# Weight and activation tiles at other byte offsets in SBUF, and high and low parts of one activation in one tile

## The chip, the cores and the metric

The kernel runs on one core of one Trainium2 chip. The metric is the device time of one execution in microseconds (us). Engines are TensorE (PE; its weight loads are shown apart as PEld), VectorE (DVE), ScalarE (ACT), GpSimd (POOL) and SyncE (SP), which issues the transfers. SBUF is the on-chip memory of 128 partitions from which PE reads both operands of a matmul; results go to PSUM. An address below is a byte offset within a partition.

## What is computed

A stack over 256 tokens of width 1,024, batch 1: one block of two mixing layers over 272 tokens (16 meta tokens in front), then two blocks of feed-forward, hybrid mixer, feed-forward, and a last norm. Cut to what matters here:

```python
def first_block(x, meta_tokens, ...):            # 16 + 256 tokens
    h = concat([meta, x]); 
    h = h + even_layer(rms_norm(h))              # latent attention + banded attention, gated, w_out
    h = h + odd_layer(rms_norm(h))               # conv + linear recurrence, gated, w_out
    return h[:, 16:]

def swiglu(x, w_gate, w_up, w_down):             # 1024 -> 2816 -> 1024, four times in all
    return (jax.nn.silu(x @ w_gate) * (x @ w_up)) @ w_down
# then twice: x += swiglu(norm(x)); x += hybrid(norm(x)); x += swiglu(norm(x))
# hybrid: causal pooling branch + gated recurrence over chunks of 64, gates and output projections
```

All inputs and the output are float32.

## The kernel before

Activations stand transposed: features on the 128 partitions, tokens along the free dimension. A projection from 1,024 features is a chain of eight tiles k of 128 features, accumulated in one PSUM bank. Each tile is multiplied with three float32r matmuls (a rounded float32 form that PE takes), so that the result keeps float32's exactness: every operand is cut into a high part and the rest, and the products are `hi·xh`, `hi·xl` and `lo·xh`, in this order (`prod`, line 447). The weights are stationary, the activation is moving:

```python
self.mm(out=out, lhsT=hi if i < 2 else lo, rhs=(xl if i == 1 else xh)[:, k, cols], ...)
```

Weights arrive by SP as `raw` buffers of 2,048 columns (two of them), and are cut into buffers of 1,024 columns, four `hi` and four `lo` (five each from the first feed-forward block's start, `more_cuts`): ACT copies `raw` to `hi`, DVE subtracts to `lo` (`cut`). Activations are cut in the same way (`split`), the normed input of a layer into `xh` and `xl`, 8 tiles of 272 tokens. From the odd layer's output on there are 256 tokens, and `place` (line 503) lays 8 tiles of 256 tokens over the same memory as `sh`, `sl`, from element 32 (`X_AT`).

The stages, in order of time: even layer (272 columns; `xh`/`xl`, the latents `lath`/`latl`, the gated heads `ysh`/`ysl` and `ymh`/`yml`); odd layer (`oyh`/`oyl`; its gates take 256 of the 272 columns); then twice feed-forward (`ffn`, line 1355: gate/up on `sh`/`sl`, down on `ph`/`pl`), hybrid (`hybrid`, line 1471: `hh`, `hl`, `hph`, `hpl`, `mh`, `ml`) and feed-forward; the final norm. In the profile the moving name stands first: `acc<-xl,hi` is a product with `xl` moving and `hi` stationary. The packed `sh`/`sl` show as `xh`, `xl`, whose memory they use. Every instruction goes through a wrapper at line 181, so lines tell nothing and names and shapes do.

The order of the instructions is set while the program is written: a clock with estimated costs (`Clock`, line 120) decides when side work, cuts and loads are put between the products. It looks at names and ranges within tiles, not at addresses. Tiles lie in SBUF one behind the other in the order in which their pool gets them, and `gap` (line 264) puts an unused tile between two to shift what follows.

Of the kernel before, what the change touches and what calls it, by code (L numbers as in the profile page):

```python
# [9 lines left out]
F32 = mybir.dt.float32  # L10
# [6 lines left out]
P = 128  # L17
D = 1024
NM = 16
S = 256  # L20
# [206 lines left out]
class Builder:  # L227

    AHEAD = 3
    X_AT = 32  # L230
    gaps = 0

    def __init__(self, ctx, tc, a):
        self.clock = Clock()
        self.ctx, self.tc, self.nc, self.a = ctx, tc, Core(tc.nc, self.clock), a
        nc = self.nc
        self.tt, self.ts, self.stt, self.ttr = nc.vector.tensor_tensor, nc.vector.tensor_scalar, nc.vector.scalar_tensor_tensor, nc.vector.tensor_tensor_reduce
        self.act, self.mm = nc.scalar.activation, nc.tensor.matmul
        self.cos, self.done, self.cur, self.lists, self.home, self.stalls = [], {}, None, {}, {}, 0
        self.loads = weight_plan()  # L240
        self.plan = [(n, i, ps, p) for n, i, ps in self.loads for p in range(len(ps))]
        self.load_at = self.conv_at = self.use_at = 0
        self.raws, self.conv = [], {}
        self.const = self.pool(ctx, "const")
        self.res = self.pool(ctx, "res", 2)
        psum = self.pool(ctx, "psum", space=PSUM)
        self.make(psum, "acc", 2, [P, 512])
        self.make(psum, "m", 6, [P, 512])
        self.make(self.const, "raw", 2, [P, 2048])
        self.make(self.const, "hi", 4, [P, 1024], F32R)  # L250
        self.make(self.const, "lo", 4, [P, 1024], F32R)
        self.make(self.const, "work", 8, [P, T + 4])
        self.make(self.const, "mx", 6, [P, 16])
# [10 lines left out]
    def gap(self, pool, n):  # L264

        if n:
            self.gaps += 1
            pool.tile([P, n // 4], F32, tag=f"gap{self.gaps}", name=f"gap{self.gaps}")

# [224 lines left out]
    def feed(self, gen, d, x, g, n):  # L494
        if n == S:
            self.place(gen)
            self.split(x, self.sh[:, d, :], self.sl[:, d, :], g)
        else:
            self.split(x, self.xh[:, d, :n], self.xl[:, d, :n], g)
        self.put("x", gen, d)  # L500
        self.spawn(self.square(gen, d, x, n))

    def place(self, gen):

        at = self.X_AT
        self.sh, self.sl = [t.rearrange("p k t -> p (k t)")[:, at:at + KD * S].rearrange("p (k t) -> p k t", t=S) for t in (self.xh, self.xl)]

# [74 lines left out]
    def setup(self):  # L582
# [8 lines left out]
        self.x = self.t(self.const, [P, KD, T], "x")  # L591
        self.xh = self.t(self.const, [P, KD, T], "xh", F32R)
        self.xl = self.t(self.const, [P, KD, T], "xl", F32R)
        nc.vector.memset(self.half, -0.5)
# [5 lines left out]
    def even(self):  # L600
# [67 lines left out]

        lath = self.t(ea, [P, 5, T], "lath", F32R)
        latl = self.t(ea, [P, 5, T], "latl", F32R)  # L670
        sums = {}
# [214 lines left out]

        ys = [self.t(ys_p, [P, 8, T], "ysh", F32R), self.t(ys_p, [P, 8, T], "ysl", F32R)]
        ym = []
# [180 lines left out]
        for h in range(8):  # L1069
            self.spawn(head(h))  # L1070
            if h == 2:
                self.need("early over")
                early.close()
                ymp = self.pool(st, "eym")
                ym += [self.t(ymp, [P, 8, T], "ymh", F32R), self.t(ymp, [P, 8, T], "yml", F32R)]
                self.put("ym")
            ps = self.take("acc")
            self.run(ein(16 + h, ps))
            self.spawn(gate(h, ps), ps)
# [21 lines left out]
    def odd(self):  # L1101
# [23 lines left out]
        def decay_rates():  # L1125
# [21 lines left out]
            self.put("c8")  # L1147

        yh = [self.t(od, [P, G, S], f"oyh{i}", F32R) for i in range(2)]
        yl = [self.t(od, [P, G, S], f"oyl{i}", F32R) for i in range(2)]  # L1150
        xcs, zgs = {}, {}
# [159 lines left out]
        for kind, g in odd_order():  # L1311
# [21 lines left out]
            else:  # L1333
                if g == 0:
                    outs += self.take("m", 4)
                    for o in outs:
                        mm(out=o, lhsT=zero, rhs=xh.rearrange("p k t -> p (k t)")[:, :512], start=True, stop=False)
                if g < 2 * NG - 2:
# [16 lines left out]
    def ffn(self, name, layer, gen, nxt):  # L1355
# [7 lines left out]
        rh = self.rh  # L1363
        self.gap(ff, 160)
        ph = self.t(ff, [P, KFF, S], "ph", F32R)
        pl = self.t(ff, [P, KFF, S], "pl", F32R)

# [61 lines left out]
    def more_cuts(self):  # L1429

        late = self.pool(self.ctx, "late")
        for n in ("hi", "lo"):
            self.lists[n].append(self.t(late, [P, 1024], n + "4", F32R))
        self.AHEAD = 4
# [36 lines left out]
    def hybrid(self, layer, gen):  # L1471
# [7 lines left out]
        hy = self.pool(st, "hy")  # L1479
        self.gap(hy, 32)  # L1480
        self.make(hy, "kq", 2, [P, H, S])
# [30 lines left out]
        pr = self.t(hy, [P, 6, S], "pr")  # L1512
        hh, hl = self.t(hy, [P, H, S], "hh", F32R), self.t(hy, [P, H, S], "hl", F32R)
        ph, pl = self.t(hy, [P, H, S], "hph", F32R), self.t(hy, [P, H, S], "hpl", F32R)

# [228 lines left out]
        for c in HYBRID:  # L1744
# [8 lines left out]
            pair(e, dst[:, e - e0:e - e0 + 2, :], (name, gen, e - e0))  # L1753

        mh, ml = self.t(hy, [P, KD, S], "mh", F32R), self.t(hy, [P, KD, S], "ml", F32R)

# [253 lines left out]
```

## Time and profile before

| | |
|---|---|
| three runs | 1537.36, 1539.48 and 1546.85 us; median 1539.48 |
| profiled execution, its own time | 1542.62 us |
| its span, first to last instruction | 1540.5 us |
| mean granted TensorE clock over the span | 0.996 |
| PE busy | 1507.8 us, 98% of the span, 12,950 instructions |
| DVE busy | 1115.9 us, 72% |
| ACT busy | 904.9 us, 59% |
| HBM read | 256.07 MB, 167 GB/s over the span |

The profile shows one execution, by instruction. Matmuls overlap: one lasts some 0.28 us, and the next starts some 0.11 us after it, so the pace is to be read from how many lie in a stretch, and not from the length of one. A granted clock of 1.00 is the 2.4 GHz level.

### The profile page before, as it was taken

Reading aid. Unit: us, or ns where it says so; the run is one execution under the profiler, and the core shown is the slowest. Engines: PE = TensorE matmul, PEld = TensorE weight load, DVE = VectorE, ACT = ScalarE, POOL = GpSimd, SP = SyncE. Lnnn points to the kernel's source line nnn. Section 1 sums busy time; section 2 is a strip of 40 time slices with the busy share of each in tenths; the row PEclk is TensorE's granted clock in tenths of the full one; section 3 lists DMA queues with packets and bytes.
Section 4 is the critical chain, followed back from the end, with each engine's and each line's share of the span. In section 5 each row is a group of like instructions: output and inputs, shape, how many; then the busy total and the mean of one; then the engine's idle time right before and its main releaser. Section 6 shows DMA issues by size and latency. Waiting matters only on the chain.

```text
span 1540.5 us, 31049 instructions
## 1 busy us (share of the span) xinstructions
PE 1507.8 (98%) x12950; PEld 1473.7 (96%) x12950; DVE 1115.9 (72%) x1882; ACT 904.9 (59%) x1435; POOL 26.2 (2%) x68
## 2 busy tenths in 40 slices
PE   8999999999989999999999999999999998999998
PEld 8989899999989999989999999999999998999998
DVE  6977775689996666668886666666666787777754
ACT  7666654699966545475455544455455754555453
POOL 1000000000000000000000000000000000000000
PEclk9999999999999999999999999999999999999999
DMA  6422224554445645644355555556456433456553
GB/s 240 152 90 83 84 81 164 182 174 143 156 174 189 218 167 183 211 161 165 137 195 189 196 177 174 194 194 214 161 188 209 167 138 137 163 189 222 175 174 117
DMA packets 42492, 259.12 MB, mean 168 GB/s; under 512 B 4840, under 2 KB 6256, under 8 KB 18416
## 3 DMA queue, kind: packets, MB, share of 16 engines
q1 hardware_dynamic: 40624, 251.90, 47.1%
q10 hardware_dynamic: 1728, 5.24, 1.0%
q8 instruction: 101, 1.65, 0.4%
q14 instruction: 39, 0.32, 0.1%
HBM read 256.07 MB, written 1.05 MB: 167 GB/s over the span
## 4 chain that ended last, share of the span: by engine, by line
PE 63%; issue 19%; DVE 10%; ACT 5%; DMA 2%; POOL 0%; POOLq 0%; ACTq 0%; SPq 0%; DVEq 0%
PE acc L181 51%; PE m L181 12%; DVE lo L181 4%; DVE big L181 3%; ACT hi L181 2%; DMA raw<-in_hin_dram 1%; ACT L181 1%; DVE kq L181 1%; ACT big L181 1%; ACT w L181 0%; DVE xc L181 0%; ACT xx L181 0%; DVE xx L181 0%; DMA raw<-in_ffn_gu_dram 0%; DVE work L181 0%
## 5 line engine op out<-in xcount | busy, mean ns | idle before, releaser
L181 DVE TENSOR_TENSOR lo<-raw,hi 128x1024 fp32r<-128x1024 f32 (+3 forms) x520 | 582.7, 1129 | 258.5 <-ACT hi L181 254.8
L181 ACT ACTIVATE hi<-raw 128x1024 fp32r<-128x1024 f32 (+3 forms) x520 | 502.2, 980 | 297.0 <-PE acc L181 207.8
L181 PE MATMUL acc<-xh,hi 128*128 128x256 f32 (+1 forms) x2096 | 589.7, 281 | 5.4 <-ACT hi L181 5.4
L181 PE MATMUL acc<-xl,hi 128*128 128x256 f32 (+1 forms) x2096 | 590.5, 282 | 0.0
L181 PE MATMUL acc<-xh,lo 128*128 128x256 f32 (+1 forms) x2096 | 588.7, 281 | 0.1
L181 PEld LDWEIGHTS acc<-xh,hi 128*128 128x128 f32 x2096 | 394.5, 188 | 6.8 <-ACT hi L181 5.4
L181 PEld LDWEIGHTS acc<-xl,hi 128*128 128x128 f32 x2096 | 395.6, 189 | 1.4
L181 PEld LDWEIGHTS acc<-xh,lo 128*128 128x128 f32 x2096 | 394.6, 188 | 1.6 <-DVE lo L181 0.5
L181 PE MATMUL acc<-pl,hi 128*128 128x256 f32 x704 | 196.9, 280 | 0.0
L181 PE MATMUL acc<-ph,lo 128*128 128x256 f32 x704 | 196.6, 279 | 0.0
L181 PE MATMUL acc<-ph,hi 128*128 128x256 f32 x704 | 196.4, 279 | 0.0
L181 PEld LDWEIGHTS acc<-pl,hi 128*128 128x128 f32 x704 | 132.2, 188 | 0.0
L181 PEld LDWEIGHTS acc<-ph,hi 128*128 128x128 f32 x704 | 132.2, 188 | 0.0
L181 PEld LDWEIGHTS acc<-ph,lo 128*128 128x128 f32 x704 | 131.8, 187 | 0.0
L181 PE MATMUL m<-xh,lo 128*128 128x256 f32 (+1 forms) x336 | 96.0, 286 | 0.0
L181 PE MATMUL m<-xl,hi 128*128 128x256 f32 (+1 forms) x336 | 95.6, 284 | 0.0
L181 PE MATMUL m<-xh,hi 128*128 128x256 f32 (+1 forms) x336 | 95.5, 284 | 0.0
L181 DVE TENSOR_TENSOR work<-acc,spread 128x256 f32<-128x256 f32 (+1 forms) x108 | 46.0, 426 | 38.0 <-PE acc L181 35.3
L181 ACT ACTIVATE work<-work 128x256 f32<-128x256 f32 (+2 forms) x92 | 37.4, 408 | 51.9 <-DVE work L181 51.5
L181 PEld LDWEIGHTS m<-xh,lo 128*128 128x128 f32 x336 | 63.6, 189 | 0.3
L181 PEld LDWEIGHTS m<-xh,hi 128*128 128x128 f32 x336 | 63.6, 189 | 0.2
L181 PEld LDWEIGHTS m<-xl,hi 128*128 128x128 f32 x336 | 63.5, 189 | 0.1
(359 smaller groups left out, 2242.4 us busy)
## 6 DMA issues: line engine op xcount, KB each, us to landing
raw<-in_ffn_gu_dram SPq DMA_DIRECT2D x88, 1024.0 KB, 4.9
raw<-in_ffn_dn_dram SPq DMA_DIRECT2D x64, 704.0 KB, 4.1
raw<-in_hin_dram SPq DMA_DIRECT2D x32, 1024.0 KB, 4.9
raw<-in_oin_dram SPq DMA_DIRECT2D x16, 1024.0 KB, 5.0
raw<-in_ein_dram SPq DMA_DIRECT2D x12, 1024.0 KB, 4.7
raw<-in_eout_dram SPq DMA_DIRECT2D x8, 1024.0 KB, 4.9
raw<-in_oout_dram SPq DMA_DIRECT2D x8, 1024.0 KB, 4.9
raw<-in_wph_dram SPq DMA_DIRECT2D x8, 1024.0 KB, 4.9
```

The costliest lines, as they stand in the source:

```text
L181: r = f(*args, **kw)
```

## The change

The instructions of every engine, their order, shapes and waits stay as they are. What changes is where tiles lie. The high and low part of one activation become two views of one tile: for 272 columns tile by tile (high k, low k, high k+1, ...), by `twins` or by the new `xs`; for 256 columns one half behind the other. Gaps shift the `lo` weight buffers by 192 bytes against the `hi` ones, and the low parts of moving operands by 64 against their high parts. The core of the diff:

```diff
         self.make(self.const, "hi", 4, [P, 1024], F32R)
+        self.gap(self.const, 192)
         self.make(self.const, "lo", 4, [P, 1024], F32R)
...
+    def twins(self, pool, shape, tag):
+
+        k, n = shape
+        t = self.t(pool, [P, k, 2, n], tag, F32R)
+        return t[:, :, 0, :], t[:, :, 1, :]
...
-        at = self.X_AT
-        self.sh, self.sl = [t.rearrange("p k t -> p (k t)")[:, at:at + KD * S].rearrange("p (k t) -> p k t", t=S) for t in (self.xh, self.xl)]
+        self.sh, self.sl = [self.xs[:, at:at + KD * S].rearrange("p (k t) -> p k t", t=S) for at in (0, KD * S + 16)]
...
-        self.xh = self.t(self.const, [P, KD, T], "xh", F32R)
-        self.xl = self.t(self.const, [P, KD, T], "xl", F32R)
+        self.gap(self.const, 192)
+        self.xs = self.t(self.const, [P, 2 * KD * T], "xs", F32R)
+        pairs = self.xs.rearrange("p (k two t) -> p k two t", two=2, t=T)
+        self.xh, self.xl = pairs[:, :, 0, :], pairs[:, :, 1, :]
...
-        lath = self.t(ea, [P, 5, T], "lath", F32R)
-        latl = self.t(ea, [P, 5, T], "latl", F32R)
+        lath, latl = self.twins(ea, (5, T), "lat")
...
-        ys = [self.t(ys_p, [P, 8, T], "ysh", F32R), self.t(ys_p, [P, 8, T], "ysl", F32R)]
+        ys = self.twins(ys_p, (8, T), "ys")
...
+        self.gap(od, 64)
         yh = [self.t(od, [P, G, S], f"oyh{i}", F32R) for i in range(2)]
+        self.gap(od, 64)
         yl = [self.t(od, [P, G, S], f"oyl{i}", F32R) for i in range(2)]
...
-        self.gap(ff, 160)
+        self.gap(ff, 96)
         ph = self.t(ff, [P, KFF, S], "ph", F32R)
+        self.gap(ff, 64)
         pl = self.t(ff, [P, KFF, S], "pl", F32R)
...
-        for n in ("hi", "lo"):
-            self.lists[n].append(self.t(late, [P, 1024], n + "4", F32R))
+        self.gap(late, 128)
+        self.lists["hi"].append(self.t(late, [P, 1024], "hi4", F32R))
+        self.gap(late, 192)
+        self.lists["lo"].append(self.t(late, [P, 1024], "lo4", F32R))
...
-        self.gap(hy, 32)
+        self.gap(hy, 96)
...
+        hh, ph, mh = [self.t(hy, [P, n, S], tag, F32R) for tag, n in (("hh", H), ("hph", H), ("mh", KD))]
+        self.gap(hy, 64)
+        hl, pl, ml = [self.t(hy, [P, n, S], tag, F32R) for tag, n in (("hl", H), ("hpl", H), ("ml", KD))]
```

Where the built programs put these tiles, as addresses modulo 256 bytes (k is the tile of 128 features; a tile of 256 columns is 1,024 bytes and one of 272 is 1,088, which is 64 more than a multiple of 256):

| operand | role | before | after |
|---|---|---|---|
| `hi` 0 to 4 | stationary | 128 | 128 |
| `lo` 0 to 4 | stationary | 128 | 64 |
| `xh`, `xl` as 256 columns | moving, gate/up and hybrid | 64, 64 | 64, 128 |
| `ph`, `pl` | moving, down | 192, 192 | 64, 128 |
| `hh`, `hph`, `mh`; `hl`, `hpl`, `ml` | moving, hybrid | 64; 64 | 64; 128 |
| `oyh`, `oyl` | moving, odd layer | 64, 64 | 64, 128 |
| `xh`, `xl` as 272 columns | moving, even and odd layer | 192+64k, 192+64k | 64+128k, 128+128k |
| `ysh`, `ysl`; `ymh`, `yml` | moving, even layer | 64+64k for all | 192+128k, 128k |
| `lath`, `latl` | moving, even layer | 64+64k, 128+64k | 192+128k, 128k |

PE's first products of the program, in the even layer, in the order in which they stand before (numbers behind a name tell its buffers apart):

```order
L181 MATMUL acc_64<-xh,hi_74 128x272
L181 MATMUL acc_64<-xl,hi_74 128x272
L181 MATMUL acc_64<-xh,lo_78 128x272
L181 MATMUL acc_65<-xh,hi_74 128x272
L181 MATMUL acc_65<-xl,hi_74 128x272
L181 MATMUL acc_65<-xh,lo_78 128x272
```

The same products after the change, on PE, where `xs` is the tile that holds both parts and x2 means two rows with the same names:

```order
L181 MATMUL acc_64<-xs,hi_74 128x272 x2
L181 MATMUL acc_64<-xs,lo_79 128x272
L181 MATMUL acc_65<-xs,hi_74 128x272 x2
L181 MATMUL acc_65<-xs,lo_79 128x272
L181 MATMUL m_66<-xs,hi_74 128x272 x2
```

Only the names differ: `xh` and `xl` have become `xs`, and `lo` buffers are numbered one higher, since a gap stands before them. The same holds where the first feed-forward block goes over from gate/up to down on PE, before:

```order
L181 MATMUL acc_65<-xh,hi_75 128x256
L181 MATMUL acc_65<-xl,hi_75 128x256
L181 MATMUL acc_65<-xh,lo_79 128x256
L181 MATMUL acc_64<-ph,hi_76 128x256
L181 MATMUL acc_64<-pl,hi_76 128x256
L181 MATMUL acc_64<-ph,lo_80 128x256
```

And after, at the same place:

```order
L181 MATMUL acc_65<-xs,hi_75 128x256 x2
L181 MATMUL acc_65<-xs,lo_80 128x256
L181 MATMUL acc_64<-ph,hi_76 128x256
L181 MATMUL acc_64<-pl,hi_76 128x256
L181 MATMUL acc_64<-ph,lo_81 128x256
```

Nothing has moved here either: three products, the same banks and the same weight buffers.

## Rows read from the trace of the kernel before

**Rows 1.** The page's first part: busy time, share of the span and instructions by engine.

```profile
PE 1507.8 (98%) x12950; PEld 1473.7 (96%) x12950; DVE 1115.9 (72%) x1882; ACT 904.9 (59%) x1435; POOL 26.2 (2%) x68
```

**Rows 2.** The page's costliest groups: busy us, mean ns | idle before, its releaser.

```profile
L181 DVE TENSOR_TENSOR lo<-raw,hi 128x1024 fp32r<-128x1024 f32 (+3 forms) x520 | 582.7, 1129 | 258.5 <-ACT hi L181 254.8
L181 ACT ACTIVATE hi<-raw 128x1024 fp32r<-128x1024 f32 (+3 forms) x520 | 502.2, 980 | 297.0 <-PE acc L181 207.8
```

**Rows 3.** Windows of PE alone in the four gate/up stages; x is the matmul count.

```profile
core 0: us, PE busy (x), PEclk, DMA share, GB/s
480.00:560.00 80.00, 80.00 (x708) 1.00 0.59 207
...
825.00:925.00 100.00, 100.00 (x852) 1.00 0.54 189
...
1010.00:1100.00 90.00, 90.00 (x797) 1.00 0.60 208
...
1370.00:1460.00 90.00, 90.00 (x796) 1.00 0.56 197
```

**Rows 4.** The same view, PE alone, in the first and last of four down stages.

```profile
585.00:635.00 50.00, 50.00 (x426) 1.00 0.58 194
...
1475.00:1525.00 50.00, 50.00 (x426) 1.00 0.51 171
```

**Rows 5.** Timeline, gate/up of the first feed-forward block: start, length (us), engine, instruction.

```profile
500.05 0.28 PE L181 MATMUL m<-xh,lo 128*128 128x256 f32 x1
500.05 0.19 PEld L181 LDWEIGHTS m<-xh,hi 128*128 128x128 f32 x1
500.16 0.28 PE L181 MATMUL m<-xh,hi 128*128 128x256 f32 x1
```

**Rows 6.** Windows of PE: even layer (272 columns), odd layer's gates, hybrid, hybrid.

```profile
235.00:285.00 50.00, 50.00 (x399) 1.00 0.53 188
314.50:325.00 10.50, 10.50 (x91) 1.00 0.29 101
708.50:720.00 11.50, 11.50 (x103) 1.00 0.11 26
755.00:810.00 55.00, 55.00 (x488) 1.00 0.54 187
```

**Rows 7.** The page's DMA issues: queue, kind, count, KB each, us to landing.

```profile
raw<-in_ffn_gu_dram SPq DMA_DIRECT2D x88, 1024.0 KB, 4.9
raw<-in_ffn_dn_dram SPq DMA_DIRECT2D x64, 704.0 KB, 4.1
raw<-in_hin_dram SPq DMA_DIRECT2D x32, 1024.0 KB, 4.9
raw<-in_oin_dram SPq DMA_DIRECT2D x16, 1024.0 KB, 5.0
...
raw<-in_oout_dram SPq DMA_DIRECT2D x8, 1024.0 KB, 4.9
raw<-in_wph_dram SPq DMA_DIRECT2D x8, 1024.0 KB, 4.9
```

**Rows 8.** PE groups by line and shape, 272 columns (of three products, one row each).

```profile
L181 PE MATMUL acc<-xh,hi 128*128 128x272 f32 x280 | 85.0, 304 | 5.4 <-ACT hi L181 5.4
...
L181 PE MATMUL m<-xh,hi 128*128 128x272 f32 x104 | 30.7, 295 | 0.0
...
L181 PE MATMUL acc<-ysh,hi 128*128 128x272 f32 x48 | 14.1, 294 | 0.0
```

**Rows 9.** Timeline, hybrid: four products of 512 columns, the first and the last.

```profile
663.74 0.39 PE L181 MATMUL m<-hi,xh 128*128 128x512 f32 x1
...
664.42 0.39 PE L181 MATMUL m<-hi,xh 128*128 128x512 f32 x1
```

**Rows 10.** Timeline, hybrid: a run of one-column matmuls, over two lengths of window.

```profile
735.63 1.39 PE L181 MATMUL m<-cst,kq 128*128 128x1 f32 x12
735.63 0.61 PE L181 MATMUL m<-cst,kq 128*128 128x1 f32 x5
```

More of the change, by code (lines that the diff above doesn't have):

```diff
@@ L229 @@
     AHEAD = 3
-    X_AT = 32
     gaps = 0
@@ L264, in gap @@
     def gap(self, pool, n):
-        if n:
-            self.gaps += 1
-            pool.tile([P, n // 4], F32, tag=f"gap{self.gaps}", name=f"gap{self.gaps}")
+        self.gaps += 1
+        pool.tile([P, n // 4], F32, tag=f"gap{self.gaps}", name=f"gap{self.gaps}")
+    def twins(self, pool, shape, tag):
+        k, n = shape
+        t = self.t(pool, [P, k, 2, n], tag, F32R)
+        return t[:, :, 0, :], t[:, :, 1, :]
     def make(self, pool, name, n, shape, dt=F32):
@@ L495, in feed @@
         if n == S:
-            self.place(gen)
+            self.place()
             self.split(x, self.sh[:, d, :], self.sl[:, d, :], g)
@@ L501, in feed, with place @@
         self.spawn(self.square(gen, d, x, n))
-    def place(self, gen):
-        at = self.X_AT
-        self.sh, self.sl = [t.rearrange("p k t -> p (k t)")[:, at:at + KD * S].rearrange("p (k t) -> p k t", t=S) for t in (self.xh, self.xl)]
+    def place(self):
+        self.sh, self.sl = [self.xs[:, at:at + KD * S].rearrange("p (k t) -> p k t", t=S) for at in (0, KD * S + 16)]
     def square(self, gen, d, x, n):
@@ L1074, in even @@
                 ymp = self.pool(st, "eym")
-                ym += [self.t(ymp, [P, 8, T], "ymh", F32R), self.t(ymp, [P, 8, T], "yml", F32R)]
+                ym += self.twins(ymp, (8, T), "ym")
                 self.put("ym")
@@ L1336, in odd @@
                     for o in outs:
-                        mm(out=o, lhsT=zero, rhs=xh.rearrange("p k t -> p (k t)")[:, :512], start=True, stop=False)
+                        mm(out=o, lhsT=zero, rhs=self.xs[:, :512], start=True, stop=False)
                 if g < 2 * NG - 2:
@@ L1512, in hybrid @@
         pr = self.t(hy, [P, 6, S], "pr")
-        hh, hl = self.t(hy, [P, H, S], "hh", F32R), self.t(hy, [P, H, S], "hl", F32R)
-        ph, pl = self.t(hy, [P, H, S], "hph", F32R), self.t(hy, [P, H, S], "hpl", F32R)
+        hh, ph, mh = [self.t(hy, [P, n, S], tag, F32R) for tag, n in (("hh", H), ("hph", H), ("mh", KD))]
+        self.gap(hy, 64)
+        hl, pl, ml = [self.t(hy, [P, n, S], tag, F32R) for tag, n in (("hl", H), ("hpl", H), ("ml", KD))]
         def memory():
@@ L1753, in hybrid @@
             pair(e, dst[:, e - e0:e - e0 + 2, :], (name, gen, e - e0))
-        mh, ml = self.t(hy, [P, KD, S], "mh", F32R), self.t(hy, [P, KD, S], "ml", F32R)
         def branch_gates():
```

## Prediction

> **What bounds the kernel now.** I read the page's busy times first: TensorE (PE) is busy 98% of a span of 1540.5 us [rows 1], so the end moves only with the pace of PE's own instructions or with its 33 us of idle time. VectorE and ScalarE come next, and they cut the weights: one pair of 1,024-column `hi`/`lo` buffers costs DVE 1.13 us and ACT 0.98 us in the mean, with 258 and 297 us of idle time ahead of such rows, in which they mostly wait for each other or for PE to free a buffer [rows 2]. A pair feeds 24 products (8 tiles of 128 columns, three products each), some 2.7 us of PE. So neither is the limit.
>
> Then I asked what pace PE keeps. The windows by stage, PE alone, give the matmuls that lie in a stretch in which PE never pauses. A matmul row is 0.28 us long while the next starts 0.11 us later [rows 5], so about 2.5 are in flight at the first instant of a window and are counted on top; I take 2.5 off each count (2.3 for 272 columns). The four gate/up stages of the feed-forward blocks issue the same 1,056 products each, from the same buffers, at a granted clock of 1.00, the 2.4 GHz level. Their paces are [rows 3]:
> - 80.00/(708−2.5) = 113.4 ns, 90.00/(797−2.5) = 113.3 and 90.00/(796−2.5) = 113.4 in three of them
> - 100.00/(852−2.5) = 117.7 ns in the second.
>
> Nothing waits there, and the second stage's DMA share (0.54) lies below that of the other three (0.56 to 0.60). So one and the same product has two paces, and a whole stage keeps one of them. The down stages are at the slow pace in all four blocks: 50.00/(426−2.5) = 118.1 [rows 4], where one matmul more or less in the count is 0.3 ns, so I put them at 117.7. What differs between up and down is where the moving operand lies: by the address table 64 bytes below the weights, modulo 256, in up (64 against 128) and 64 above them in down (192 against 128). In the 272-column stage, where the moving operand walks through all four quarters from tile to tile, a product takes 50.00/(399−2.3) = 126.0 ns [rows 6]. 256 columns at 2.4 GHz are 106.7 ns and 272 are 113.3, so what stands over the columns is 6.7, 11.0 and 12.7 ns. The timeline shows what could collide: the next LDWEIGHTS starts within some ns of each MATMUL [rows 5], so one tile's moving rows and the next tile's weights are read from SBUF at once. I read the two paces as this collision, and placement as what the change is about.
>
> **The change part by part.** No engine gets an instruction more or less, none changes place or shape, and no wait is added: the order of the two kernels differs in names only. So every term is pace. The work: a 1,024 KB weight transfer is 16 weight tiles of 128 columns, 48 products; one of 704 KB is 11, 33 products [rows 7]. Gate/up: 88×48 = 4,224. Down: 64×33 = 2,112. The other 256-column products: (32+8+16+8)×48 = 3,072. With 272 columns: 3×(280+104) on `x` and 6×48 on `ys`/`ym`, 1,440 [rows 8].
>
> After the change the moving operand of one product and the weights that are loaded under it stand, product by product, 64 below (`xh` while the `hi` of the second product is loaded), 64 above (`xl` while `lo` is loaded) and 64 below (`xh` while the next `hi` is loaded). They are never level, and the sign changes from product to product. In before it is the same sign for every product of a stage, and the trace shows a stage that stays slow for all of its products. I take it that a slow pace needs the same relation again and again, so that the alternation ends it, and price every 256-column product at the fast pace, 113.4 ns. This step is an inference; its other ends are the rivals.
> - Down stages, 2,112×(117.7−113.4) = −9.1 us.
> - The second gate/up stage, 1,056×4.3 = −4.5 us; the three others nothing.
> - The other 3,072: their three windows give 10.50/(91−2.5) = 118.6, 11.50/(103−2.5) = 114.4 and 55.00/(488−2.5) = 113.3 [rows 6], mean 115.4; 3,072×2.0 = −6.1 us.
> - The 1,440 of 272 columns. Best case: a 512-column product takes (664.42−663.74)/3 = 227 ns [rows 9], so a column costs (227−117.7)/256 = 0.43 ns and 16 columns 6.8, and 113.4+6.8 = 120.2 ns. Worst case: 126.0 as now, since the tiles still walk, now in steps of 128 over two quarters. No row is nearer to either; I take the middle, 123: −4.3 us (ends 0 and −8.4).
> - The 156 latent products and the few with operands exchanged: below 1 us either way, nothing.
>
> Sum −24.0. The profiled execution took 1542.62 us, so 1518.6 on its scale; it stands 3.1 above the median of 1539.48, so about 1516 against that median.
>
> The cutting hides under this as before: 24 products at 113.4 ns are 2.72 us against 1.13 and 0.98. Transfers too: a 1,024 KB raw buffer per 48 products (5.4 us) is what three gate/up stages already drew, 207 GB/s without a pause [rows 3]. If that cover were gone, PE would show idle time before `hi` or `lo`. The gaps cost room and no instruction.
>
> **Rivals.**
> *Little or nothing moves.* If each product's pace goes by its own pair alone, two of three pairs are like up in before (113.4) and one like down (117.7): 114.8 everywhere. Then down and the second gate/up stage gain 3,168×2.9 = 9.2, the rest 3,072×0.6 = 1.8, and the other three lose 3,168×1.4 = 4.4; −6.6 us, about 1533. For it: up and down do differ by this sign. Against it: the second gate/up stage had the same sign as the other three. In the same case belongs that SBUF placement does nothing and the two paces come from elsewhere, an order of start-up for instance that holds for a stage: 1539.5. For that: the one stage with two paces at the same addresses. The Trainium skill has a rule of this kind: "SBUF — State Buffer", section "SBUF: two separate sides", says that of the engines only the pair of ports shared with GpSimd causes contention and that "PE, ACT, and DVE's dedicated pair never wait on anyone". By that rule the time would stay 1539.5; the trace bears on it only in that one product has two paces at full clock with nothing waiting, which the rule leaves without a cause.
>
> *Slower.* The stationary and moving reads of one product are now level in two of three: `xl` lies on the quarter of `hi` and `xh` on that of `lo` (128 and 64). In before the feed-forward stages have no level product. If the product's own pair counts and not the next load, the alternation locks every product at the slow pace. Three gate/up stages then lose 3,168×4.3 = 13.6 us and the rest 3,072×2.3 = 7.1: +20.7, about 1560. It decides once more than two thirds of these products run at 117.7. A pace as far over the columns as that of the 272-column stage (106.7+12.7 = 119.4) would add 9,408×1.7 = 16 us, 1576. For it: the 272-column work and the odd layer's gates (the 118.6 above), whose tiles walk, are the only ones that pass the level relation, and are the slowest of their widths. Against it: by [rows 5] it is the next load that runs beside a product, and those pairs are never level.
>
> *Much faster.* Weight loads alone take (1.39−0.61)/7 = 111.4 ns each (columns of one element, 12 of them against 5) [rows 10], so a product can't be paced below that. If all reached it: 2,112×6.3+1,056×6.3+3,168×2.0+3,072×4.0 = 38.6 us, and 1,440×(126−118.2) = 11.2: about 1490. No window is nearer to 111.4 than 113.3.
>
> **How the numbers follow.** Fast pace nearly everywhere 0.41, the much faster case 0.04; little 0.20 and nothing 0.14; slower 0.21. About 1%, 15 us, is what a measurement of this kernel can tell from no change, so faster means below 1524 and slower above 1555. The first two give faster 0.45, the next two same 0.34, the last slower 0.21. The time is that of the likeliest case, 1516, whose own range is 1500 (every 256-column product between 113.4 and 111.4, the 272 at their best) to 1524. The whole range reaches from 1500 to 1560, the slower case's first mark, and leaves out 0.04 below and about 0.12 above.
>
> **What would show it.** The same stages in the new trace: at 113.4 ns a 50 us window in a down stage holds some 443 matmuls where 426 stand now, and a 100 us window of the second gate/up stage 884 for 852; 440 to 430 speak for the mixture, unchanged counts for no effect, fewer in the three other gate/up stages for the slower case. In the 272-column stage 50 us should hold some 409 (418 at best). DVE and ACT rows should keep their means. It is wrong if stages still fall to either pace with no regard to address, or if idle time before `hi` and `lo` grows.

## The result, and the profile after

The changed kernel takes 1559.49 us in the median of four runs (1558.47 to 1559.92), the kernel before 1540.15 beside it (1537.36 to 1546.85): a ratio of 1.0118, 95% interval [1.0085, 1.0151]. It is 1.2% slower. The forecast was 1516 us, with a range of 1500 to 1560 that ends half a microsecond above the median; the time lies where the rival *Slower* put it, about 1560.

The page of the kernel after, its first part (busy time, share of the span, instructions), and its two costliest cutting groups:

```profile
PE 1527.1 (98%) x12950; PEld 1493.5 (96%) x12950; DVE 1115.7 (72%) x1882; ACT 904.7 (58%) x1435; POOL 26.1 (2%) x68
...
L181 DVE TENSOR_TENSOR lo<-raw,hi 128x1024 fp32r<-128x1024 f32 (+3 forms) x520 | 582.1, 1128 | 258.5 <-ACT hi L181 246.3
L181 ACT ACTIVATE hi<-raw 128x1024 fp32r<-128x1024 f32 (+3 forms) x520 | 502.0, 980 | 305.6 <-PE acc L181 207.5
```

Against [rows 1] PE has the same 12,950 instructions and is busy 19 us longer; its idle time fell by 2 us (1557.6−1527.1 = 30.5 for 32.7). DVE and ACT cut at the means of [rows 2], 1128 ns for 1129 and 980 for 980; ACT idles 9 us more ahead of its copies (305.6 for 297.0). So PE waits no longer than before: it runs at another pace itself.

Windows of the kernel after, PE alone, same columns as before (busy time, matmul count, granted clock, DMA share, GB/s). In order: the four gate/up stages with a down stage behind each of the first and fourth, then the even layer's 272 columns, the odd layer's gates and a hybrid stretch.

```profile
core 0: us, PE busy (x), PEclk, DMA share, GB/s
480.00:560.00 80.00, 80.00 (x682) 1.00 0.56 198
585.00:635.00 50.00, 50.00 (x427) 1.00 0.53 175
825.00:925.00 100.00, 99.93 (x849) 1.00 0.57 197
...
1010.00:1100.00 90.00, 90.00 (x766) 1.00 0.56 196
...
1370.00:1460.00 90.00, 89.92 (x764) 1.00 0.54 189
1490.00:1540.00 50.00, 50.00 (x427) 1.00 0.52 175
...
235.00:285.00 50.00, 50.00 (x404) 1.00 0.56 190
314.50:325.00 10.50, 10.50 (x91) 1.00 0.28 100
...
755.00:810.00 55.00, 55.00 (x468) 1.00 0.47 168
```

Read as in the prediction, 2.5 matmuls in flight taken off: 80.00/(682−2.5) = 117.7 ns in the first gate/up stage where [rows 3] gave 113.4, 90.00/(766−2.5) = 117.9 in the third, 118.1 and 118.2 in the second and fourth, where PE paused for some 0.1 us. The down stages stay where they were in [rows 4], 50.00/(427−2.5) = 117.8. The hybrid stretch goes from 113.3 [rows 6] to 118.2, and the odd layer's gates keep their count of 91. Only the 272-column work gained: 50.00/(404−2.3) = 124.5 ns for 126.0. The granted clock is 1.00 in all of them. Every feed-forward stage of the changed kernel runs at one pace, about 117.8 ns (one matmul more or less is 0.15 to 0.3 ns in these windows), while before some ran at 113.4.

Three gate/up stages lose 3,168×4.4 = 13.9 us, and the products of 272 columns give back 1.5 ns each. There are 1,536 of these: the prediction's 1,440 leave out 96 on `ys` and `ym` that write to `m` banks (16 of each of six forms). That is 2.3 us. PE's busy time grew by 1527.1−1507.8 = 19.3, which leaves 19.3−13.9+2.3 = 7.7 us, 2.5 ns a product, for the 3,072 others; this is a remainder and not read from windows. With 2.2 us less of idle time the spans differ by 1557.6−1540.5 = 17.1.

### The profile page after: what moved, and what is told of

The parts are those of the page before. It is cut to its first block, busy times and chain, and to the rows that moved or that the text cites. A ratio compares the mean times of both kernels' runs of the same rounds, so it can differ in the third digit from the quotient of the medians.

```text
span 1557.6 us, 31049 instructions
## 1 busy us (share of the span) xinstructions
PE 1527.1 (98%) x12950; PEld 1493.5 (96%) x12950; DVE 1115.7 (72%) x1882; ACT 904.7 (58%) x1435; POOL 26.1 (2%) x68
## 4 chain that ended last, share of the span: by engine, by line
PE 68%; issue 18%; DVE 8%; ACT 4%; DMA 1%; POOL 0%; POOLq 0%; ACTq 0%; SPq 0%; DVEq 0%
PE acc L181 54%; PE m L181 14%; DVE lo L181 3%; DVE big L181 2%; ACT hi L181 1%; DVE kq L181 1%; DMA raw<-in_hin_dram 1%; ACT L181 1%; ACT big L181 1%; DVE xc L181 1%; DVE work L181 0%; ACT xx L181 0%; DVE xx L181 0%; ACT w L181 0%; DVE lf L181 0%
## 5 line engine op out<-in xcount | busy, mean ns | idle before, releaser
L181 PE MATMUL acc<-xs,hi 128*128 128x256 f32 (+1 forms) x4192 | 769.0, 285 | 5.7 <-ACT hi L181 5.7
L181 DVE TENSOR_TENSOR lo<-raw,hi 128x1024 fp32r<-128x1024 f32 (+3 forms) x520 | 582.1, 1128 | 258.5 <-ACT hi L181 246.3
L181 ACT ACTIVATE hi<-raw 128x1024 fp32r<-128x1024 f32 (+3 forms) x520 | 502.0, 980 | 305.6 <-PE acc L181 207.5
L181 PEld LDWEIGHTS acc<-xs,hi 128*128 128x128 f32 x4192 | 643.4, 188 | 8.3 <-ACT hi L181 5.7
L181 PE MATMUL acc<-xs,lo 128*128 128x256 f32 (+1 forms) x2096 | 588.4, 281 | 0.0
L181 PEld LDWEIGHTS acc<-xs,lo 128*128 128x128 f32 x2096 | 402.6, 192 | 1.3 <-DVE lo L181 0.2
L181 PE MATMUL m<-xs,hi 128*128 128x256 f32 (+1 forms) x672 | 126.5, 287 | 0.0
L181 PEld LDWEIGHTS m<-xs,hi 128*128 128x128 f32 x672 | 104.4, 190 | 0.4
L181 PE MATMUL m<-xs,lo 128*128 128x256 f32 (+1 forms) x336 | 96.1, 286 | 0.0
L181 PEld LDWEIGHTS m<-xs,lo 128*128 128x128 f32 x336 | 64.7, 193 | 0.3
L181 ACT ACTIVATE ph<-work 128x256 fp32r<-128x256 f32 x88 | 35.9, 410 | 28.6 <-DVE work L181 28.1
L181 DVE TENSOR_TENSOR pl<-work,ph 128x256 fp32r<-128x256 f32 x88 | 36.6, 419 | 10.2 <-ACT ph L181 10.2
```

Of the source, the lines that this page charges most:

```text
L181: r = f(*args, **kw)
```

## The experiments

Below, a relation is the address of the moving operand minus that of the weights, modulo 256 bytes. Three theories stood after the result. **A** is the rival of the prediction: a product suffers when its moving operand is level with its own weights. **B**: it suffers when the moving operand stands 64 above the weights that are loaded under it, which in the changed kernel is the case once in three products. **C**: it suffers when the relation to the next weights changes from product to product. In before, stages were seen at 113.4 or 117.8 ns where every relation is −64, and only at 117.8 where every one is +64; A and C alone give no reason for the second. The diffs below are shortened, and where a run gives all stages one value, that value stands in place of the table by stage.

**The down stages at the place of gate/up.** Before, with `ph` and `pl` 64 below the weights:

```diff
-        self.gap(ff, 160)
+        self.gap(ff, 32)
```

> Only ph and pl move, from 192 to 64, so that the down stages too have their moving operand 64 below the weights; all else as before. Theory A (a product is slow when its moving operand is level with its own weights), theory B (slow when the moving operand lies 64 above the weights that are loaded under it) and theory C (slow when that relation changes from product to product) all expect the down stages to leave 117.8 ns: 113.4 in those that follow a gate/up stage at 113.4 (first, third, fourth) and 117.8 after the second, 3x528x4.4 = 7 us, about 1533. If the down stages are slow for a reason other than address, they stay at 117.8 and the time at 1540.

1532.29 us against 1542.66, ratio 0.9945 [0.9914, 0.9977]. Windows of this kernel, first block's gate/up and down, then the fourth block's:

```profile
480.00:560.00 80.00, 80.00 (x708) 1.00 0.60 205
590.00:630.00 40.00, 40.00 (x356) 1.00 0.59 186
...
1375.00:1450.00 75.00, 75.00 (x640) 1.00 0.57 197
1488.00:1522.00 34.00, 34.00 (x291) 1.00 0.41 139
```

The down stage of the first block now runs at 40.00/(356−2.5) = 113.2 ns, as do those of the second and third (356 in 40 us each). In the fourth block gate/up fell to 75.00/(640−2.5) = 117.6, at the addresses at which it ran at 113.4 in [rows 3], and its down stage took that over, 117.9. So address is what kept the down stages back, and at −64 there are two paces; in this trace each gate/up stage hands its pace on to the down stage behind it.

**Each offset alone.** Before, with only the `lo` weights moved (and a gap behind them that leaves all else in place; `lo4` likewise):

```diff
+        self.gap(self.const, 192)
         self.make(self.const, "lo", 4, [P, 1024], F32R)
+        self.gap(self.const, 64)
```

> Only the lo weight buffers move, from 128 to 64; moving operands as before (x at 64, ph and pl at 192). In gate/up the product xh lo is now level with its own weights, and xl is level with the lo weights loaded under it. A: every gate/up stage at 117.8, about 1540+14+5 = 1559 with the hybrid work. B: nothing stands 64 above its next weights in gate/up, so three of four stages can keep 113.4 and the time stays at 1540. C: the relation changes twice in three products, so all at 117.8, 1559.

Before, with only the low moving parts of feed-forward and hybrid inputs (`xl`) and of down (`pl`) 64 above their high parts, `X_AT` being a pair of elements for the two, and `ph` at 64:

```diff
-    X_AT = 32
+    X_AT = (32, 48)            # elements: xh at 64, xl at 128
-        self.gap(ff, 160)
+        self.gap(ff, 32)
...
+        self.gap(ff, 64)
         pl = self.t(ff, [P, KFF, S], "pl", F32R)
```

> Only the low moving parts move: xl to 128 and the down stages to ph 64, pl 128; weights as before, both at 128. xl hi is level with its own weights, and xl with the lo weights loaded under it. A: gate/up and down at 117.8, about 1555. B: no product stands 64 above its next weights, so gate/up may hold 113.4 and down comes to it, 1531 to 1540. C: 117.8 everywhere, about 1555.

The first took 1562.29 us, ratio 1.0132 [1.0107, 1.0156], the second 1564.99, 1.0154 [1.0123, 1.0185]. Either offset alone costs about as much as both together, the second some 10 us more than the 1555 expected. Windows of the kernel with the `lo` offset: gate/up and down of the first block, gate/up of the third.

```profile
480.00:560.00 80.00, 80.00 (x681) 1.00 0.59 202
590.00:630.00 40.00, 40.00 (x349) 1.00 0.59 196
...
1010.00:1090.00 80.00, 80.00 (x657) 1.00 0.54 186
```

Windows of the kernel with the offset of the low moving parts, gate/up and down of the first block and gate/up of the second:

```profile
480.00:560.00 80.00, 80.00 (x681) 1.00 0.57 201
590.00:630.00 40.00, 40.00 (x342) 1.00 0.58 197
835.00:915.00 80.00, 80.00 (x673) 1.00 0.57 198
```

117.9 and 122.2 ns in gate/up of the first, 117.9 and 119.3 in the second. Neither has a moving operand 64 above its next weights in gate/up, and still no stage of theirs is at 113.4, so B falls as the only cause. A new pace shows in the down stages of the first: 40.00/(349−2.5) = 115.4, with `ph` and `pl` at 192, `hi` at 128 and `lo` at 64.

**Many pairs of addresses in one kernel.** `place` and `ffn` were given addresses by stage, eight pairs in a run; the weights lie as stated.

```diff
-        at = self.X_AT
...
+        self.sh, self.sl = [... for t, at in zip((self.xh, self.xl), self.X_AT[gen])]
...
+        at = {2: (32, 64), 4: (224, 64), 5: (160, 64), 7: (96, 64)}[gen]
+        self.gap(ff, at[0])
         ph = self.t(ff, [P, KFF, S], "ph", F32R)
+        self.gap(ff, at[1])
```

> The lo weights at 192, hi at 128, and another pair of moving addresses (high, low part) in each stage: gate/up (64,128), (64,64), (64,192), (64,0) in the four blocks, down (64,128), (0,64), (192,0), (128,192). What the trace tells is the pace of each stage; the whole time is not the point. Moving minus next weights, in order of the three products: gate/up -64 -64 -64; -64 -128 -64; -64 0 -64; -64 +64 -64. Down: -64 -64 -64; -128 -128 -128; +64 +64 +64; 0 0 0. Expected at 117.8 ns or more: A (own pair level) gate/up of block 1, down of blocks 1, 3 and 4. B (64 above the next weights) gate/up of block 4 and down of block 3 alone. C (a change from product to product) gate/up of blocks 2, 3 and 4, and of down none but block 3, whose like is slow in the kernel before.

> Weights as before, hi and lo both at 128. In each stage high and low moving parts share one address, another one per stage, so that the relation to the weights is the same for all three products. Moving minus weights: gate/up 0, 128, -32 and -96 in the four blocks; down +32, +96, 0 and 128. So far only -64 has shown 113.4 ns (beside 117.8), and +64 only 117.8. Theory F (any constant relation but a few has the pace of 113.4): most of these stages show 113.4. Theory G (of the steps of 64 only -64 has it): 0 and 128 show 115.6 or more, and the odd steps of 32 tell how wide the good place is.

> Weights as before, both at 128; high and low moving parts at two addresses. Gate/up (64,0), (64,128), (64,192), (0,0); down (64,0), (128,128), (0,0), (64,192). If the pace is lost whenever the three products don't share one relation (theory C, kept for the fast pace alone), all the mixed pairs show 115.6 ns or more, with 117.8 the likeliest; if only some mixtures lose it, one of (64,0) and (64,192) shows 113.4. The constant ones (0,0) and (128,128) repeat relations of the kernel with constant ones in other stages and should show the same pace in either place, if address and not stage decides.

Each window gives its time over the count less 2.5, as above; of the third kernel three stages are shown. One matmul more or less is 0.35 ns in a window of 40 us and 0.17 in one of 80. Windows with `lo` at 192, gate/up and down of the four blocks in turn:

```profile
480.00:560.00 80.00, 80.00 (x677) 1.00 0.57 199
590.00:630.00 40.00, 40.00 (x340) 1.00 0.58 193
835.00:915.00 80.00, 80.00 (x679) 1.00 0.55 194
940.00:980.00 40.00, 40.00 (x337) 1.00 0.53 179
1010.00:1090.00 80.00, 80.00 (x694) 1.00 0.55 188
1128.00:1168.00 40.00, 40.00 (x342) 1.00 0.53 174
1400.00:1460.00 60.00, 60.00 (x512) 1.00 0.58 206
...
1488.00:1522.00 34.00, 34.00 (x291) 1.00 0.57 185
```

Windows with one relation for all three products, the same stages without the last down stage:

```profile
480.00:560.00 80.00, 80.00 (x669) 1.00 0.57 193
590.00:630.00 40.00, 40.00 (x342) 1.00 0.56 182
835.00:915.00 80.00, 80.00 (x676) 1.00 0.56 194
940.00:980.00 40.00, 40.00 (x335) 1.00 0.54 179
1010.00:1090.00 80.00, 80.00 (x679) 1.00 0.54 185
1128.00:1168.00 40.00, 40.00 (x337) 1.00 0.55 180
1400.00:1460.00 60.00, 60.00 (x508) 1.00 0.59 203
```

Windows with both weights at 128 and mixed pairs: gate/up of the first block, down of the second with (128, 128), gate/up of the third.

```profile
480.00:560.00 80.00, 80.00 (x676) 1.00 0.57 198
...
940.00:980.00 40.00, 40.00 (x336) 1.00 0.54 181
1010.00:1090.00 80.00, 80.00 (x682) 1.00 0.57 198
```

| `lo` weights | moving, high and low part | relation to the next weights, three products | ns |
|---|---|---|---|
| 128 | 64, 64 | −64, −64, −64 | 113.4 or 117.8 |
| 128 | 192, 192 | +64, +64, +64 | 117.8 |
| 128 | 128, 128 | 0, 0, 0 | 120.0 |
| 128 | 0, 0 | 128, 128, 128 | 118.7 or 120.3 |
| 128 | 96, 96 | −32, −32, −32 | 118.3 |
| 128 | 32, 32 | −96, −96, −96 | 118.7 |
| 128 | 160, 160 | +32, +32, +32 | 117.8 |
| 128 | 224, 224 | +96, +96, +96 | 120.3 |
| 128 | 64, 0 | −64, 128, −64 | 118.8 |
| 128 | 64, 128 | −64, 0, −64 | 117.9 or 119.3 |
| 128 | 64, 192 | −64, +64, −64 | 117.7 |
| 192 | 64, 128 | −64, −64, −64 | 118.6 |
| 192 | 64, 64 | −64, −128, −64 | 118.3 |
| 192 | 0, 64 | −128, −128, −128 | 119.6 |
| 192 | 64, 192 | −64, 0, −64 | 115.7 |
| 192 | 64, 0 | −64, +64, −64 | 117.8 |
| 192 | 192, 0 | +64, +64, +64 | 117.8 |
| 192 | 128, 192 | 0, 0, 0 | 117.9 |
| 64 | 64, 64 | −64, 0, −64 | 117.9 or 122.2 |
| 64 | 192, 192 | +64, 128, +64 | 115.4 |
| 64 | 64, 128 (the change) | −64, +64, −64 | 117.8 |

All three theories fall as the only cause. The pair (64, 64) with `lo` at 192 has no level product and is not at the better pace (118.3), against A, and so it is with twelve more pairs of the table. The pair (64, 128) with `lo` at 192 has the relation −64 to the next weights three times and is at 118.6: nothing stands 64 above, against B, and nothing changes from product to product, against C. Of the two theories in the second expectation F falls, and G holds: of the constant relations only −64 has the better pace, and 32 bytes to either side of it (118.3 at −32, 118.7 at −96) it is gone. What is left is narrower: in these 21 arrangements of 256-column products, 113.4 ns showed only where `hi`, `lo` and both moving parts keep one relation of −64. The three stages with (128, 128), one in gate/up and two in down of two kernels, are at 119.6 to 120.0, so address decides here and not the stage; (0, 0) shows two paces again, and neither is 113.4. Two limits stand beside this. Ten of the 21 were seen in one stage only, and as a placement can have two paces, a better one there is not excluded. And `hi` stood at 128 in every run, so that it is the difference of 64 that counts, and not the two places 64 and 128 themselves, is not shown.

**What chooses between the two paces at −64.** Before, with `ph` at 64 and an extra matmul ahead of each of the last 18 pairs of gate and up chains:

```diff
+            width = {2: 1, 4: 32, 5: 64, 7: 128}[gen]
+            if e0 >= 4:
+                bank = self.take("m")
+                mm(out=bank[:, :width], lhsT=self.c("ones"), rhs=self.c("ident")[:, :width], start=True, stop=True)
+                self.drop(bank)
```

> ph and pl at 64, and in each gate/up stage an extra plain float32 matmul into a free bank ahead of each of the last 18 pairs of gate and up chains, 1, 32, 64 and 128 columns wide in the four blocks (its result is not used). With -64 throughout, two paces have been seen, and the stage changes between them where the norm's small matmuls come in. If an interruption is what chooses the pace, stretches of 48 products at 113.4 and at 117.8 alternate, with changes only at the extra matmuls, and a block's width decides which comes. If the pace is a property of the stage or of the time of day of the run, it doesn't change at them. The time is up by some 72 interruptions of 0.1 to 0.3 us and by what the paces make of it: 1545 to 1565.

Timeline of this kernel in the first block's gate/up stage, the extra matmuls alone (start in us; each shows as two rows, x2, and 48 products lie between one and the next):

```profile
480.59 0.28 PE L181 MATMUL m<-cst 128*128 128x1 f32 x2
...
486.47 0.28 PE L181 MATMUL m<-cst 128*128 128x1 f32 x2
...
492.16 0.28 PE L181 MATMUL m<-cst 128*128 128x1 f32 x2
...
498.04 0.28 PE L181 MATMUL m<-cst 128*128 128x1 f32 x2
```

The steps are 5.88, 5.69 and 5.88 us, and so on through all 18. Each extra matmul turns the pace over, and it stays until the next one; 5.88−5.69 = 0.19 us over 48 products is the 4 ns between the paces. The second block, with 32 columns, kept 113.4 after every one of its 18. The same kernel with widths in the order 1, w, w (w = 32, 16, 48, 96 in the four blocks):

```diff
+                width = {2: (1, 32, 32), 4: (1, 16, 16), 5: (1, 48, 48), 7: (1, 96, 96)}[gen][(e0 - 4) % 3]
```

> As the kernel with extra matmuls in the gate/up stages, all at -64, but the widths come in the order 1, w, w, again and again, with w = 32, 16, 48 and 96 in the four blocks. Width 1 has changed the pace each time. If an extra matmul of 32 columns leaves the pace as it is, the stretches of block 1 go in the order slow slow slow, fast fast fast (a width of 1 turning it over, 32 keeping it). If 32 columns bring the better pace from either side, the order is slow fast fast. The other widths tell which of the two each of them is. As no width in this rests on an earlier run but 1 and 32, no time is forecast beyond 1535 to 1565.

Timeline of its first block's gate/up stage, the extra matmuls alone:

```profile
480.98 0.28 PE L181 MATMUL m<-cst 128*128 128x1 f32 x2
...
486.86 0.30 PE L181 MATMUL m<-cst 128*128 128x32 f32 x2
...
492.55 0.30 PE L181 MATMUL m<-cst 128*128 128x32 f32 x2
...
498.24 0.28 PE L181 MATMUL m<-cst 128*128 128x1 f32 x2
```

5.88, then 5.69 and 5.69: after width 1 the worse pace, after either 32 the better one. The fourth block, with 96 columns, does the same:

```profile
1376.26 0.28 PE L181 MATMUL m<-cst 128*128 128x1 f32 x2
...
1382.14 0.35 PE L181 MATMUL m<-cst 128*128 128x96 f32 x2
...
1387.83 0.36 PE L181 MATMUL m<-cst 128*128 128x96 f32 x2
...
1393.51 0.28 PE L181 MATMUL m<-cst 128*128 128x1 f32 x2
```

In the other two blocks 16 did as 32, bringing 113.4 from either side, and 48 turned the pace over as 1 had, and as 64 and 128 had in the kernel with one width a block. So at −64 the pace is chosen by the last interruption of the stream. The kernel before has such places too. In its second gate/up stage two products and the norm's matmuls of one column stand so:

```profile
806.46 0.28 PE L181 MATMUL m<-xh,lo 128*128 128x256 f32 x1
...
812.92 0.28 PE L181 MATMUL m<-xh,lo 128*128 128x256 f32 x1
...
814.00 0.61 PE L181 MATMUL m<-cst,acc 128*128 128x1 f32 x4 [0.69 <-DVE acc L181]
```

The two products are 57 apart: (812.92−806.46)/57 = 113.3 ns. Behind the norm's matmuls the starts lie 117.8 ns apart, the pace of [rows 3]. That it is these matmuls, with the 0.69 us that PE waits ahead of them, is taken over from the extra ones; no run here moved them alone.

**The 272-column tiles.** Before with `ph` at 64, and `ymh` and `yml` tiles 320 columns apart, so that half of the even layer's output products keep −64 and the others walk:

```diff
-                ym += [self.t(ymp, [P, 8, T], "ymh", F32R), self.t(ymp, [P, 8, T], "yml", F32R)]
+                ym += [self.t(ymp, [P, 8, 320], tag, F32R)[:, :, :T] for tag in ("ymh", "yml")]
```

> ph and pl at 64 as in the kernel with the down stages below the weights, and the tiles of ymh and yml 320 columns apart instead of 272, so that each of their 272-column products stands 64 below its weights, while ysh and ysl still walk through the four quarters. If the walk is what costs, ymh and yml products go from 126.1 ns to 120 (113.4 and 16 columns more) or, in the second lock, 124.5, and ysh and ysl stay at 126.1: 192 products, -0.3 to -1.2 us. If 272 columns are slow for their length alone, nothing moves. The time 1531 to 1533 either way.

1530.89 us against 1539.08, ratio 0.9955 [0.9928, 0.9983]. Nearly all of that is the step of `ph` to 64, which alone gave 0.9945; the padding is worth some 0.5 us (192 products at 2.5 ns). The window of this kernel to be set against the 399 of [rows 6]:

```profile
235.00:285.00 50.00, 50.00 (x403) 1.00 0.55 190
```

50.00/(403−2.3) = 124.8 ns over a stretch of which half is padded; with the walking half at 126.0 as before the padded products come to 123.5. So part of what 272 columns cost over 256 is the walk, 2.5 ns a product; the 123.5 lies between the two paces of the expectation, 120 and 124.5.

**The change without its offsets.** The changed kernel, tiles interleaved as it has them, but every 256-column operand at −64:

```diff
-        self.gap(self.const, 192)
         self.make(self.const, "lo", 4, [P, 1024], F32R)
...
-        self.sh, self.sl = [... for at in (0, KD * S + 16)]
+        self.sh, self.sl = [... for at in (0, KD * S)]
...
         ph = self.t(ff, [P, KFF, S], "ph", F32R)
-        self.gap(ff, 64)
```

> The changed kernel without its two offsets: lo weights back at 128 like hi, low moving parts level with their high parts (x, ph and pl, the odd layer's and the hybrid's tiles all at 64). The interleaved 272-column tiles stay. If the offsets among the three products are what cost the changed kernel its time, the gate/up and down stages come to 113.4 ns where the pace is the better of the two, and the time to about 1530, some 30 us below the changed kernel. If moving the tiles together into one tile is what costs, the stages stay at 117.8 and the time above 1550. The 272-column products: 124.5 ns if interleaving alone brought the 1.6 ns, 126.1 if the lo offset did.

1536.26 us (1526.85 to 1544.05, ten runs) against 1542.11, ratio 0.9973 [0.9954, 0.9993]. The profiled execution is the fastest of the ten (1526.85 us), and all eight feed-forward stages in it are at the better pace; windows of gate/up and down of the first block, and the 272 columns:

```profile
480.00:560.00 80.00, 80.00 (x708) 1.00 0.60 211
590.00:630.00 40.00, 40.00 (x355) 1.00 0.58 191
...
235.00:285.00 50.00, 50.00 (x403) 1.00 0.54 189
```

The offsets are what cost the changed kernel its time; one tile for both parts costs nothing that these times can tell. The median is some 6 us above the 1530 expected. The 272 columns, with `lo` back at 128, are at 124.8 ns, so most of the gain there (124.5 in the changed kernel, 126.0 before) is the interleaving's. But the times spread over 17 us, where those of the changed kernel, whose feed-forward stages have one pace only, spread over 1.5 in four runs.

**The better pace on purpose.** The same kernel, with one extra matmul of 96 columns in six places: in each gate/up stage once the norm's matmuls are by, and ahead of each hybrid's last product stage.

```diff
+    def relock(self):
+        bank = self.take("m")
+        self.mm(out=bank[:, :96], lhsT=self.c("ones"), rhs=self.c("ident")[:, :96], start=True, stop=True)
+        self.drop(bank)
...
+            if e0 == 4:
+                self.relock()
```

> The interleaved kernel at -64, with one extra plain float32 matmul of 96 columns into a free bank (its result is not used) in each of six places: in the four gate/up stages after the norm's own matmuls have gone by, and ahead of the hybrids' last product stage. 96 columns brought 113.4 ns from either pace. If the pace that a stage happens to fall into is what spreads the times of the level kernel from 1526.9 to 1544.1 us, this kernel has the better pace in all eight feed-forward stages in every execution: a median of about 1526 to 1528, six extra matmuls included, and a spread of 5 us or less. If the spread has another source, the median stays near 1536 and the spread near 15 us.

1528.87 us (1526.84 to 1533.26, six runs) against 1541.78, ratio 0.9919 [0.9896, 0.9942]: 0.8% below the kernel before and about 2% below the changed one. The median is 7 us under the level kernel's, and all eight feed-forward stages of the profiled execution are at the better pace (708 matmuls in 480:560, 356 in 590:630). Both marks of the first expectation, a median of 1526 to 1528 and a spread of 5 us or less, are just missed: the spread is 6.4 us, where the other expectation was near 15. So the chance pace of the feed-forward stages is the likeliest source of most of the level kernel's spread. It is not seen directly, since none of that kernel's slower executions was profiled; and what the rest is, other places where a pace can change (the odd layer, the hybrids) or something else, no run here tells.

## Why the prediction was wrong

**What bounds the kernel** was right. PE was the limit and remained so, the cutting and the transfers kept up at either pace, and the change acted by pace alone. That placement bears on the pace was right too, and the rival by which placement does nothing is out, with the time of 1539.5 that it gave: the same instructions lost 4.4 ns each in three whole stages. That the time lies inside the range is no merit of the sum, whose own range ended at 1524; the upper end was the rival *Slower*'s first mark.

**The step that failed** is the sentence "I take it that a slow pace needs the same relation again and again, so that the alternation ends it". It was put on the reading that a stage stays slow for all of its products, and that was not quite so: the second gate/up stage began at 113.3 ns and changed at 814 us, ahead of the window from 825 that was read. And it turned the reading the wrong way round. It is the better pace that needed the same relation again and again. Of 21 arrangements it showed in one, and that was the one that the kernel before already had in gate/up and hybrid. The worse paces came under all the others, constant or mixed. Every term of the sum but the last rested on that step:
- *Down stages*, −9.1 us forecast, nothing came, since (64, 128) with `lo` at 64 is at 117.8 as (192, 192) was. The term's size was right for another edit: moved to 64 without offsets, three of four down stages gained 4.5 ns a product, and the whole kernel 0.55%.
- *The second gate/up stage*, −4.5 us forecast, nothing came. That it stood at 117.7 in [rows 3] had no cause in its addresses, since it began at 113.3 with the same ones, but by all signs in the interruption by the norm's matmuls; with the down stages moved it was the fourth that stood there, and in the execution profiled with the tiles interleaved at −64 none.
- *The other 3,072 products*, −6.1 us forecast, about +7.7 came, by the remainder.
- *The three gate/up stages at 113.4*, forecast to stay, lost 13.9 us. This is the largest part of the miss.
- *272 columns*, −4.3 us forecast, −2.3 came: 124.5 ns where the middle of my bounds was 123. The direction was right, and the size about half of the forecast; the 96 products left out change it by 0.1 us.

**The rival *Slower*** had the time (1560 for 1559.5), the stages and their price (13.6 us for 13.9, and 7.1 for about 7.7 in the rest). Its cause, a product level with its own weights, was not the one: thirteen arrangements without any level product ran at 115.4 to 120.3 ns. So the rival was right in its number and not in its reason. Its chance of 0.21 was low all the same. The trace of before spoke for it in two places that I had read: 113.4 was read only where all relations were −64, and the products that passed through several relations (272 columns, the odd layer's gates) were the ones furthest from their column time. The change left the one arrangement that was seen at the better pace for one that was seen nowhere, and 20 of the 21 arrangements don't have that pace.

**The rival by which each pair has its own price** (114.8 everywhere, 1533) falls as well: paces don't mix linearly, and one pair of three changed takes the stage to a worse pace as a whole.

**Still open**: why −64 has the better pace, and what is late in the worse ones. Whether the weights in use or those loaded under a product count can't be told apart either; −64 to the next ones alone is not enough (118.6). Addresses were compared modulo 256 bytes only: +64 and −64 are the same modulo 128 and differ, and no larger modulus was tried. Five of the paces lie on even steps: 113.4, 115.6, 117.8, 120.0 and 122.2 ns are 2.2 apart (115.6 showed as 115.4 and 115.7 by the counts), and at the granted 2.4 GHz 3×2.2×2.4 is 16 cycles in three products. 118.3 to 118.8 don't lie on these steps, and what takes the cycles no run here shows.

## What to carry to other kernels

When a stream of matmuls is near its limit, count matmuls in windows by stage, because equal shapes at an equal clock can run at two paces, and their difference (4% here) shows in no wait and no idle time. Keep the arrangement of addresses that the trace shows at the better pace and bring the other stages to it, one at a time, rather than to a new arrangement that looks better by argument. If a pace can be lost by an interruption, look for what interrupts; a kernel whose runs spread by 1% while nothing in it waits may be changing between paces.

## What the runs showed of the hardware that was not expected

- Where the moving operands of float32r matmuls stand against the weights, modulo 256 bytes, moves the pace of 256-column products between 113.4 and 122.2 ns at a granted clock of 1.00, with no idle time on PE. (`hi` weights at 128 in all runs.)
- At one and the same placement there are two steady paces, 113.4 and 117.8 ns, and one plain float32 matmul of a single column between the products turns the one into the other: 48 products take 5.88 us after one such matmul, and 5.69 after the next. Other placements showed two paces as well, 118.7 and 120.3 at (0, 0) for one.
- The width of the interrupting matmul decides: 16, 32 and 96 columns of plain float32 brought the better pace from either side, 1, 48, 64 and 128 turned it over, each 12 times or more.
- A pace is handed on: with gate/up and down both at −64, down ran at 113.2 ns behind three gate/up stages at 113.4, and at 117.9 behind one at 117.6.
